# A hybrid encoder layer on one core: zero tile for the clock-raising passes, x rows first, and four blocks' queries normalised where they are used

## The chip, the cores and the metric

The kernel runs on one core of a Trainium2 chip. The time is the device time of one execution in microseconds; "before" and "after" are compared by it. The profile is that of one execution: TensorE (PE, with its weight loads PEld), VectorE (DVE), ScalarE (ACT), GpSimd (POOL) and SyncE (SP), whose queue issues the DMA transfers here. Each engine works through its own queue in order.

## The reference

One encoder layer with two head groups beside each other, on a prompt of 256 rows and a sample of 2048, each with 16 learned meta rows in front; the model dimension is 1024.

```python
h = rmsnorm(z, norm_w)
proj = jnp.einsum('bld,de->ble', h, w_in)
q, k, v, g_att, c_val, c_glu, g_conv = jnp.split(proj, SPLIT_IDX, axis=-1)
q = rmsnorm(q.reshape(B, L, N_HEADS, HEAD_DIM), q_norm_w)      # 8 heads of 64
k = rmsnorm(k.reshape(B, L, N_KV_HEADS, HEAD_DIM), k_norm_w)   # 2 KV heads
att = windowed_gqa(q, k, v, sink).reshape(B, L, W_ATT) * jax.nn.silu(g_att)
cnv = conformer_conv(c_val, c_glu, conv_w, conv_b, ln_w, ln_b) * jax.nn.silu(g_conv)
mixed = jnp.concatenate([att, cnv], axis=-1)
return z + jnp.einsum('ble,ed->bld', mixed, w_out)             # residual
```

`windowed_gqa` lets a row see the keys at a distance of at most 128 (with a penalty on the distance), all 16 meta keys, and a sink logit; `conformer_conv` is a GLU, a depthwise convolution of width 31, a layer norm over channels and a swish. Everything is float32.

## The kernel before

**Tiling.** The rows are cut into 18 blocks of 128 (2 of the prompt, 16 of the sample), in 6 groups of 3. A float32 product is made of three passes on TensorE (`PASSES`: high by high, high by low, low by high), so operands are split into a high part (`xh`, `ws`) and a low part (`xl`).

**Stages.** Up to about 550 us the projections run, one weight unit after the other over the row groups, with the convolution on VectorE beside them (`pj<-xh,ws`, `y<-us,cw,y`). Then attention and output projection run, one step per block and eight slots per step (`slot_step`), at first merged with the last projections: in each step the scores `S` of one block, the transposes `pT` and the weighted sums `O` of the block before it, and parts of the output products into two PSUM banks `yb0` and `yb1`. `add` in `product` adds a finished bank to a tile `yo` that holds the residual rows (`load_x`) or a partial sum; a bank goes on accumulating for the next output after that, so the next matmul into it has to come behind the add.

**Order.** A list scheduler with a simulated timeline sets the order on each engine, except for instructions kept in program order (`pinned`, `pin`, `keep_in_program_order`), and except that GpSimd, and in the last part TensorE too, follow an order written by hand. `later(k, f)` puts work off by k ticks. All DMAs are issued on SP's queue. They use eight semaphores in turn.

**The start.** `stats(i)` loads the rows `xn0` (16 meta rows) to `xn3` and takes their mean squares; POOL makes 1/rms of them and VectorE multiplies. TensorE transposes them (`turn0`, `xt<-ident,xn`). Between these, `busy` runs passes that only keep TensorE at work, 10, 5, 2 and 3 of them ahead of the rows 0 to 3, each of two records in the trace, on the identity matrix, which POOL makes. ScalarE then multiplies by the norm weights, held in `vec` (`split0`, `xh<-xt,vec`).

**Queries.** `q_group` makes the queries of a block, half of the heads (256 columns) at a time. In the merged stage ScalarE copies the raw product out of PSUM (`qr<-pj`), the 1/rms of each head (`rqq`) is worked out, and `fin` multiplies on VectorE (`qr<-qr,rqq`) and stores to the DRAM buffer `qd` (`qd<-qr`). For the second half of the last four blocks, 14 to 17, `fin` is put off by `put_off` (16 to 34 ticks), past the projections. In the attention stage, `load_q` loads a block's queries from `qd` (`q<-qd`), and `q_prep` transposes them (`qT`) and splits them.

Of the kernel before, what the change touches and what calls it, by code (L numbers as in the profile page):

```python
# [11 lines left out]
F32 = mybir.dt.float32  # L12
# [3 lines left out]
ALU = mybir.AluOpType  # L16
AX = mybir.AxisListType

P = 128
# [10 lines left out]
HD = 64  # L30
# [3 lines left out]
UW = 256  # L34
# [23 lines left out]
VSLOT = 3  # L58
# [83 lines left out]
def hymba_kernel(  # L142
# [11 lines left out]
    nc = tc.nc  # L154
# [5 lines left out]
    qd = dram.tile([NB, P, 512], F32, name="qd")  # L160
# [9 lines left out]
    ident = const.tile([P, P], F32, name="ident")  # L170
    make_identity(nc, ident)
    vec = const.tile([P, 30], F32, name="vec")
# [3 lines left out]
    lb = vec[:, 16:20]  # L176
    snk, msk, nsnk = vec[:, 22:24], vec[:, 24:28].rearrange("p (k i) -> p k i", k=2), vec[:, 28:30]
    vm = const.tile([P, 2, KV, P], F32R, name="vm")
    km = const.tile([P, KV, 2, NM], F32R, name="km")
    half = const.tile([P, 8], F32, name="half")  # L180
    nc.vector.memset(half, -0.5)
# [14 lines left out]
    def owe(ns):  # L196
        credit[0] -= ns

    def later(k, f):
        due.setdefault(clock[0] + k, []).append(f)  # L200
# [47 lines left out]
    kscale = cp.tile([P, 1], F32, tag="kscale", name="kscale", bufs=1)  # L248
# [106 lines left out]
    def load_v(b):  # L355
        vt[b] = [
            pool["a"].tile([P, KV, P], F32R, tag=f"v{k}", name=f"v{k}_{b}", bufs=VBUFS)
            for k in ("c", "m", "a", "b")[: 4 if kind(b) == "in" else 2]
        ]
        t = [x.rearrange("p a e -> p (a e)").bitcast(F32) for x in vt[b]]  # L360
        if kind(b) != "in":
            at = b - (kind(b) == "last")
            for k in range(2):
                nc.sync.dma_start(t[k], vd[at + k])
            return
        nc.sync.dma_start(t[0][QB:P], vd[b, 0 : P - QB])
        nc.sync.dma_start(t[0][0:QB], vd[b - 1, QC : QC + QB])
        nc.sync.dma_start(t[1][0:QB], vd[b, P - QB : P])
        nc.sync.dma_start(t[1][QB:QC], vd[b - 1, P - QB : P])
        nc.sync.dma_start(t[1][QC:P], vd[b + 1, 0:QC])  # L370
        nc.sync.dma_start(t[2][0:QC], vd[b - 1, 0:QC])
        nc.sync.dma_start(t[2][QC:XR], vmd)
        nc.sync.dma_start(t[3][0:NM], vmd)
        nc.sync.dma_start(t[3][NM:XR], vd[b + 1, QC:P])

    def load_q(b):
        qt[b] = pool["a"].tile([P, 4, P], F32, tag="q", name=f"q{b}")
        nc.sync.dma_start(qt[b].rearrange("p a e -> p (a e)"), qd[b])

    def presplit_wo(e):  # L380

# [105 lines left out]
    def pin(on):  # L487
        def wrap(f):
            def g(*a, **k):
                r = f(*a, **k)  # L490
                if on:
                    tc.keep_in_program_order(r)
                return r

            return g

        return wrap
# [319 lines left out]
    def slot_step(s_, slot):  # L817
        a, bb = s_, s_ - 1
        has_a, has_b = a < NB, 0 <= bb < NB
        steps = PLAN if has_b else []  # L820
        if slot == 0:
            if a + 1 < NB:
                load_q(a + 1)
                load_k(a + 1)
        if slot == 1 and has_b and s_ > 1:
            load_ga(bb)
        if slot == VSLOT and 0 < a < NB:
            load_v(a)
        t = 8 * s_ + slot
        with_rest(lambda: None)  # L830
        for f in acts.get(t, ()):
            f()
        if slot < len(steps) and steps[slot]:
            bank(bb, *steps[slot])
        for job in jobs.get(t, ()):
            product(*job)
        if has_a:
            scores(a, slot // 4, slot % 4)
        if slot == (3 if s_ == 1 else 5 if s_ == 3 else QSLOT) and a + 1 < NB:
            q_prep(a + 1)  # L840
        for job in late_jobs.get(t, ()):
            product(*job)
        tick(2400)
# [44 lines left out]
    if True:  # L888
# [3 lines left out]
        def pinned(op, yes=True):  # L892
            if yes:
                tc.keep_in_program_order(op)
# [294 lines left out]
        def q_group(ws, qi, g, after):  # L1189
            for b in range(3 * g, 3 * g + 3):  # L1190
                ps = proj_te(ws, g, blk_local(b)[1], P)
                late = phase[0] == 2
                raw = None
                tail = max(0, last_n[0] - (LTAGS_N - 4))
                put_off = 10 + 6 * tail if tail else 0
                if late:
                    raw = gp.tile([P, 4, HD], F32, tag="go" if b % 2 else "qs", name=f"qr{qi}_{b}")
                    nc.scalar.copy(raw, ps[:, :UW].rearrange("p (h e) -> p h e", e=HD))
                rq = head_norm(ps, P, 4, f"q{qi}_{b}", 2 * late + put_off)

                def fin(ps=ps, rq=rq, b=b, raw=raw):
                    tag = "go" if phase[0] == 2 and b % 2 else "qs"
                    qs = raw if raw is not None else gp.tile([P, 4, HD], F32, tag=tag, name=f"qs{qi}_{b}")
                    pin(late and not put_off)(nc.vector.tensor_tensor)(
                        qs,
                        qs if raw is not None else ps[:, :UW].rearrange("p (h e) -> p h e", e=HD),
                        rq.unsqueeze(2).to_broadcast([P, 4, HD]),
                        op=ALU.mult,
                    )
                    to = qd[b, :, UW * qi : UW * qi + UW]  # L1210
                    later(2 - late, lambda: nc.sync.dma_start(to, qs.rearrange("p h e -> p (h e)")))

                owe(340)
                later(1 + 2 * late + put_off, fin)
                tick(24 * 110)
                after(b)

# [70 lines left out]
        def busy(pt, n):  # L1288

            for _ in range(n):  # L1290
                tc.keep_in_program_order(nc.tensor.matmul(pt[:, :P], ident, ident, start=True, stop=True))  # L1291

        def turn0(i, d):

# [18 lines left out]
        preps = [Prep(g, False) for g in range(6)]  # L1313
        w01 = [weights(k) for k in range(2)]
        r = {0: stats(0)}
        nc.sync.dma_start(vec[:, 0:28], vecs)
        for i in (1, 2, 3):
            r[i] = stats(i)
        w01[0][0](nc.sync)
        w01[1][0](nc.sync)  # L1320
        nc.sync.dma_start(cw, conv_w)
        warmup = psum.tile([P, 512], F32, tag="a", name="warmup")
        for i in range(4):
            r[i]()
            o, rows = SEGS0[i]
            pinned(nc.vector.tensor_scalar(rows0[i][:rows], rows0[i][:rows], rstd[:rows, i : i + 1], None, op0=ALU.mult))
            busy(warmup, (10, 5, 2, 3)[i])
            for d in range(6):
                tc.keep_in_program_order(turn0(i, d))
        preps[0].alloc()  # L1330
# [10 lines left out]
                for i in range(4):  # L1341
                    turn0(i, 6 + q)

        nc.vector.tensor_scalar(nsnk, snk, -1.0, None, op0=ALU.mult)
        nc.vector.scalar_tensor_tensor(kscale, vec[:, 20:21], -(HD ** -0.5), vec[:, 21:22], op0=ALU.mult, op1=ALU.mult)

        def at_item_start(i, c, u, g):
            if (c, u, g) == (1, ORDER[0], CHUNKS[1][1]):
                nc.sync.dma_start(km.bitcast(F32), kmd)
                for r0 in range(0, P, NM):  # L1350
                    at = vm[r0 : r0 + NM, r0 // 64]
                    nc.sync.dma_start(at.rearrange("p a e -> p (a e)").bitcast(F32), vmd)
            if i == 6:
                nc.gpsimd.memset(vm.bitcast(F32), 0.0)
            if i == 0:
                for q in range(4):
                    w01[1][1](q, nc.gpsimd if q % 2 else nc.vector)
                for k in (4, 5, 6):
                    r[k]()
            if i == 1:  # L1360
                later(1, preps[1].first)
                later(1, preps[1].alloc)
                later(1, lambda: preps[1].scale(0))
                for q in range(4):
                    if q < 3:
                        later(1, lambda q=q: preps[1].scale(q + 1))
                    later(1, lambda q=q: preps[1].split(q))
                later(1, lambda: conv(0, U_C[0], 0))
                for k in range(7, 10):
                    later(1, lambda k=k: later(1, stats(k)))  # L1370
                for q in range(4):
                    later(2, lambda q=q: preps[2].load(q))
            if i == I2:
                later(1, preps[2].first)
                later(1, preps[2].alloc)
                later(1, lambda: preps[2].scale(0))
                for q in range(4):
                    if q < 3:
                        later(1, lambda q=q: preps[2].scale(q + 1))
                    later(1, lambda q=q: preps[2].split(q))  # L1380
                later(1, lambda: conv(0, U_C[1], 0))
# [17 lines left out]
        for i, (c, u, g) in enumerate(items):  # L1399
# [39 lines left out]
            if (c, u) == (0, ORDER[-1]):  # L1439
                p = preps[g + 3]  # L1440
# [85 lines left out]
```

## Time and profile before

| | us |
|---|---|
| runs | 933.9, 935.42, 935.51; median 935.42 |
| the profiled execution | 935.46, its span 933.4 |
| PE busy | 926.0 (99%) |
| DVE busy | 786.3 (84%) |
| ACT busy | 447.6 (48%) |
| POOL busy | 350.5 (38%) |

The span runs from the first to the last instruction of the core; the time has 2.06 us more around it. A row of the timeline gives the start and the length in us, engine, line, operation, output<-inputs and shapes, and in brackets how long the engine stood idle before it and for whom. A row of a table of stretches gives the stretch, its length, the busy time of PE, PEld, DVE, ACT and POOL (with counts), the granted clock of TensorE, the DMA engines' share and GB/s. "DMA to landing" is the time from a transfer's issue on SP until its data are there.

### The profile page before, as it was taken

Reading aid. Unit: us, or ns where it says so; the run is one execution under the profiler, and the core shown is the slowest. Engines: PE = TensorE matmul, PEld = TensorE weight load, DVE = VectorE, ACT = ScalarE, POOL = GpSimd, SP = SyncE. Lnnn points to the kernel's source line nnn. Section 1 sums busy time; section 2 is a strip of 40 time slices with the busy share of each in tenths; the row PEclk is TensorE's granted clock in tenths of the full one; section 3 lists DMA queues with packets and bytes.
Section 4 is the critical chain, followed back from the end, with each engine's and each line's share of the span. In section 5 each row is a group of like instructions: output and inputs, shape, how many; then the busy total and the mean of one; then the engine's idle time right before and its main releaser. Section 6 shows DMA issues by size and latency. Waiting matters only on the chain.

```text
span 933.4 us, 16976 instructions
## 1 busy us (share of the span) xinstructions
PE 926.0 (99%) x5742; PEld 877.0 (94%) x5742; DVE 786.3 (84%) x1380; ACT 447.6 (48%) x1237; POOL 350.5 (38%) x538
## 2 busy tenths in 40 slices
PE   9999999999999999999999999999999999999998
PEld 8999999999999999999999999988888888888887
DVE  5799999989988899999996564689788888887884
ACT  7441222153447750011111356677667676776772
POOL 3420100075675310000000453676664556455652
PEclk9999999999999999999999999999999999999999
DMA  8579685488465472223333688998566566576431
GB/s 299 181 226 360 243 287 186 156 272 311 121 211 176 155 290 91 91 99 110 117 116 116 196 268 265 384 361 251 169 171 187 169 200 167 171 187 190 139 96 47
DMA packets 154183, 182.79 MB, mean 196 GB/s; under 512 B 48784, under 2 KB 114656, under 8 KB 153968
## 3 DMA queue, kind: packets, MB, share of 16 engines
q1 hardware_dynamic: 154096, 181.71, 60.0%
q8 instruction: 45, 0.74, 0.3%
q14 instruction: 42, 0.34, 0.1%
HBM read 115.81 MB, written 65.85 MB: 195 GB/s over the span
## 4 chain that ended last, share of the span: by engine, by line
PE 97%; DVE 1%; ACT 1%; POOL 1%; issue 0%; DVEq 0%; POOLq 0%
PE pj L1050 43%; PE yb L755 20%; PE pj L1066 16%; PE O L644 5%; PE S L490 4%; PE pT_c L610 2%; PE pT_m L610 2%; PE pT_x L610 1%; PE warmup L1291 1%; PE lnu L287 1%; PE lnt L263 1%; PE qT L490 1%; PE xt L1298 0%; DVE xt L959 0%; DVE y L1131 0%
## 5 line engine op out<-in xcount | busy, mean ns | idle before, releaser
L1050 PE MATMUL pj<-xh,ws 128*128 128x384 f32 (+1 forms) x1536 | 395.4, 338 | 0.1
L1131 DVE SCALAR_TENSOR_TENSOR y<-us,cw,y 128x1167 f32<-128x1167 f32 (+2 forms) x258 | 333.5, 1348 | 0.9
L1050 PEld LDWEIGHTS pj<-xh,ws 128*128 128x128 f32 x1536 | 280.9, 188 | 0.4 <-ACT xh L1306 0.4
L1050 PE MATMUL pj<-xl,ws 128*128 128x384 f32 (+1 forms) x768 | 261.4, 341 | 0.2 <-DVE xl L988 0.2
L1066 PE MATMUL pj<-ws,xh 128*128 128x256 f32 (+1 forms) x880 | 165.4, 284 | 0.7 <-ACT sqq L1179 0.4
L1050 PEld LDWEIGHTS pj<-xl,ws 128*128 128x128 f32 x768 | 144.3, 188 | 0.5 <-DVE xl L988 0.5
L1066 PEld LDWEIGHTS pj<-ws,xh 128*128 128x128 f32 (+1 forms) x880 | 136.5, 187 | 1.4 <-issue 1.0
L755 PE MATMUL yb<-wo,rest 128*128 128x512 f32 (+1 forms) x498 | 132.9, 400 | 0.5 <-DVE rest L490 0.5
L1066 PE MATMUL pj<-ws,xl 128*128 128x256 f32 (+1 forms) x440 | 123.8, 281 | 0.0
L755 PEld LDWEIGHTS yb<-wo,rest 128*128 128x128 f32 x498 | 86.8, 189 | 16.0 <-DVE rest L490 0.9
L580 POOL TENSOR_SCALAR sb<-sb,es 128x304 f32<-128x304 f32 (+4 forms) x144 | 73.0, 525 | 58.4 <-PE pT_x L610 20.6
L1165 ACT ACTIVATE go<-pj 128x384 f32<-128x384 f32 x48 | 23.5, 490 | 147.4 <-PE pj L1050 143.2
L185 POOL TENSOR_SCALAR ssk<-ssk 128x2 f32<-128x2 f32 x18 | 11.8, 657 | 208.2 <-ACT sqk L1179 205.2
L562 ACT ACTIVATE sb<-sb,nm 128x304 f32<-128x304 f32 (+4 forms) x144 | 77.2, 536 | 22.1 <-DVE nm L550 20.2
L550 DVE CUSTOM_DVE_ANT_0 sb<-S,bias,vec 128x304 f32<-128x304 f32 (+4 forms) x144 | 73.3, 510 | 11.4 <-PE S L490 10.4
L1066 PEld LDWEIGHTS pj<-ws,xl 128*128 128x128 f32 (+1 forms) x440 | 82.1, 187 | 0.3
L185 POOL TENSOR_SCALAR ssq<-ssq 128x4 f32<-128x4 f32 (+2 forms) x55 | 27.9, 507 | 99.3 <-ACT xn L913 72.8
L490 PEld LDWEIGHTS S<-kw,q 128*128 128x128 f32 x288 | 52.2, 188 | 11.1 <-ACT rest L490 0.3
L490 PE MATMUL S<-kw,q 128*128 128x304 f32 (+4 forms) x288 | 62.3, 299 | 0.0
L755 PE MATMUL yb<-wo,ptiles 128*128 128x512 f32 x216 | 59.9, 407 | 0.0
L490 POOL TENSOR_TENSOR at<-at,ga 128x256 f32<-128x256 f32 x36 | 27.0, 750 | 79.0 <-DVE at L666 79.0
L766 DVE TENSOR_TENSOR yo<-yb,yo 128x512 f32<-128x512 f32 (+1 forms) x55 | 37.1, 674 | 14.7 <-PE yb L755 14.5
(166 smaller groups left out, 1439.7 us busy)
## 6 DMA issues: line engine op xcount, KB each, us to landing
wd<-ws SPq DMA_DIRECT2D x36, 512.0 KB, 5.8
ws<-wd SPq DMA_DIRECT2D x36, 512.0 KB, 6.1
wraw<-in_w_in SPq DMA_DIRECT2D x52, 256.0 KB, 6.3
xn<-in_z SPq DMA_DIRECT2D x18, 512.0 KB, 5.3
gd<-go SPq DMA_DIRECT2D x48, 192.0 KB, 2.9
yo<-in_z SPq DMA_DIRECT2D x36, 256.0 KB, 3.4
wo<-wod SPq DMA_DIRECT2D x18, 512.0 KB, 7.7
out_y<-yo SPq DMA_DIRECT2D x35, 256.0 KB, 2.3
```

Source lines behind the costliest of these rows:

```text
L185: nc.gpsimd.tensor_scalar(src, src, scale, eps, op0=ALU.mult, op1=ALU.add)
L490: r = f(*a, **k)
L550: nc.vector.tensor_tensor_reduce(out=sb[:, n, c0:c1], in0=ps[:, 0:w], in1=cst["bias"][:, kv, at + c0 : at + c1], scale=1.0, scalar=nsnk[:, ...
L562: nc.scalar.activation(sb[:, n, c0:c1], sb[:, n, c0:c1], AF.Exp, bias=nm[:, n : n + 1], scale=-1.0, accum_out=rs[:, n : n + 1],)
L580: nc.gpsimd.tensor_scalar(sb[:, k, a0:a1], sb[:, k, a0:a1], es[:, k : k + 1], 1.0, op0=ALU.mult, op1=ALU.mult)
L610: nc.tensor.transpose(pt[: c1 - c0, n, :], sbt[b, kv][:, n, c0:c1], ident)
L644: nc.tensor.matmul(opj[b, kv][:, n0:n1], t, p, start=(k == "c" and i == 0), stop=(k == "x" and i == len(work) - 1),)
L755: nc.tensor.matmul(ps[:, :n], x[mi][:, i, :], w[wi], start=((name, e) in OPENS and k == 0), stop=(done and e == es[-1] and k == 2), skip_g ...
L766: nc.vector.tensor_tensor(y, ps[:, :n], y, op=ALU.add)
L1050: nc.tensor.matmul(ps[:, :n], ws[:, d, wi, P * half_i : P * half_i + P], x[xi][:, d, o : o + n], start=(k == 0), stop=(k == 3 * ND - 1),)
L1066: nc.tensor.matmul(ps[:rows, :UW], x[xi][:, d, o : o + rows], ws[:, d, wi, :], start=(k == 0), stop=(k == 3 * ND - 1),)
L1131: op = nc.vector.scalar_tensor_tensor(y[:, yo + o0 : yo + o1], u[:, o0 + k : o1 + k], cw[:, j, k : k + 1], y[:, yo + o0 : yo + o1], op0=AL ...
```

## The change

- The passes of `busy` read `idle`, 128x128 elements of the tile `vm`, which VectorE sets to zero as its first work. The first group has 15 passes instead of 10 (30 records instead of 20). The memset of `vm` on POOL covers the remaining 384 columns and is pinned to a later place.
- On SP the load of `vec` stands behind the four loads of x rows. The two operations that make `nsnk` and `kscale` of it are pinned.
- For the second half of blocks 14 to 17, `keep` stores the raw queries one tick after the copy, and `rqq` is kept. `scale_q` multiplies on VectorE, in place, in the tile that `load_q` has loaded. `fin` and its multiply are not used for these four.

```diff
--- before.py
+++ after.py
@@ -176,6 +176,8 @@
     lb = vec[:, 16:20]
     snk, msk, nsnk = vec[:, 22:24], vec[:, 24:28].rearrange("p (k i) -> p k i", k=2), vec[:, 28:30]
     vm = const.tile([P, 2, KV, P], F32R, name="vm")
+    idle = vm[:, 0, 0].bitcast(F32)
+    nc.vector.memset(idle, 0.0)
     km = const.tile([P, KV, 2, NM], F32R, name="km")
     half = const.tile([P, 8], F32, name="half")
     nc.vector.memset(half, -0.5)
@@ -376,6 +378,13 @@
     def load_q(b):
         qt[b] = pool["a"].tile([P, 4, P], F32, tag="q", name=f"q{b}")
         nc.sync.dma_start(qt[b].rearrange("p a e -> p (a e)"), qd[b])
+
+    raw_q = {}
+
+    def scale_q(b):
+        qi, rq = raw_q[b]
+        q = qt[b].rearrange("p a e -> p (a e)")[:, UW * qi : UW * qi + UW].rearrange("p (h e) -> p h e", e=HD)
+        nc.vector.tensor_tensor(q, q, rq.unsqueeze(2).to_broadcast([P, 4, HD]), op=ALU.mult)
 
     def presplit_wo(e):
 
@@ -826,6 +835,8 @@
             load_ga(bb)
         if slot == VSLOT and 0 < a < NB:
             load_v(a)
+        if slot == VSLOT and a + 1 in raw_q:
+            scale_q(a + 1)
         t = 8 * s_ + slot
         with_rest(lambda: None)
         for f in acts.get(t, ()):
@@ -1201,7 +1212,7 @@
                 def fin(ps=ps, rq=rq, b=b, raw=raw):
                     tag = "go" if phase[0] == 2 and b % 2 else "qs"
                     qs = raw if raw is not None else gp.tile([P, 4, HD], F32, tag=tag, name=f"qs{qi}_{b}")
-                    pin(late and not put_off)(nc.vector.tensor_tensor)(
+                    pin(late)(nc.vector.tensor_tensor)(
                         qs,
                         qs if raw is not None else ps[:, :UW].rearrange("p (h e) -> p h e", e=HD),
                         rq.unsqueeze(2).to_broadcast([P, 4, HD]),
@@ -1210,8 +1221,15 @@
                     to = qd[b, :, UW * qi : UW * qi + UW]
                     later(2 - late, lambda: nc.sync.dma_start(to, qs.rearrange("p h e -> p (h e)")))
 
+                def keep(rq=rq, b=b, raw=raw):
+                    nc.sync.dma_start(qd[b, :, UW * qi : UW * qi + UW], raw.rearrange("p h e -> p (h e)"))
+                    raw_q[b] = (qi, rq)
+
                 owe(340)
-                later(1 + 2 * late + put_off, fin)
+                if put_off:
+                    later(1, keep)
+                else:
+                    later(1 + 2 * late, fin)
                 tick(24 * 110)
                 after(b)
 
@@ -1288,7 +1306,7 @@
         def busy(pt, n):
 
             for _ in range(n):
-                tc.keep_in_program_order(nc.tensor.matmul(pt[:, :P], ident, ident, start=True, stop=True))
+                tc.keep_in_program_order(nc.tensor.matmul(pt[:, :P], idle, idle, start=True, stop=True))
 
         def turn0(i, d):
 
@@ -1313,9 +1331,9 @@
         preps = [Prep(g, False) for g in range(6)]
         w01 = [weights(k) for k in range(2)]
         r = {0: stats(0)}
-        nc.sync.dma_start(vec[:, 0:28], vecs)
         for i in (1, 2, 3):
             r[i] = stats(i)
+        nc.sync.dma_start(vec[:, 0:28], vecs)
         w01[0][0](nc.sync)
         w01[1][0](nc.sync)
         nc.sync.dma_start(cw, conv_w)
@@ -1324,7 +1342,7 @@
             r[i]()
             o, rows = SEGS0[i]
             pinned(nc.vector.tensor_scalar(rows0[i][:rows], rows0[i][:rows], rstd[:rows, i : i + 1], None, op0=ALU.mult))
-            busy(warmup, (10, 5, 2, 3)[i])
+            busy(warmup, (15, 5, 2, 3)[i])
             for d in range(6):
                 tc.keep_in_program_order(turn0(i, d))
         preps[0].alloc()
@@ -1341,8 +1359,12 @@
                 for i in range(4):
                     turn0(i, 6 + q)
 
-        nc.vector.tensor_scalar(nsnk, snk, -1.0, None, op0=ALU.mult)
-        nc.vector.scalar_tensor_tensor(kscale, vec[:, 20:21], -(HD ** -0.5), vec[:, 21:22], op0=ALU.mult, op1=ALU.mult)
+        pinned(nc.vector.tensor_scalar(nsnk, snk, -1.0, None, op0=ALU.mult))
+        pinned(
+            nc.vector.scalar_tensor_tensor(
+                kscale, vec[:, 20:21], -(HD ** -0.5), vec[:, 21:22], op0=ALU.mult, op1=ALU.mult
+            )
+        )
 
         def at_item_start(i, c, u, g):
             if (c, u, g) == (1, ORDER[0], CHUNKS[1][1]):
@@ -1351,7 +1373,7 @@
                     at = vm[r0 : r0 + NM, r0 // 64]
                     nc.sync.dma_start(at.rearrange("p a e -> p (a e)").bitcast(F32), vmd)
             if i == 6:
-                nc.gpsimd.memset(vm.bitcast(F32), 0.0)
+                pinned(nc.gpsimd.memset(vm.bitcast(F32).rearrange("p h k e -> p (h k e)")[:, P:], 0.0))
             if i == 0:
                 for q in range(4):
                     w01[1][1](q, nc.gpsimd if q % 2 else nc.vector)
```

The new order changes on four engines. On SP, in the stage where the last projections run beside the first attention steps, the rows are, before from the load of `gc2` on, and then after, from behind the first wo2 transfer on (`wo` are split weights of the output projection, `wod` their buffer in DRAM, `yo1<-in_z` a load of residual rows; "x2" is two transfers in a row):

```order
L467 DMA gc2_6987<-gd_64 128x4x128
L457 DMA wo2_6597<-wod_71 128x1024 x2
L1211 DMA qd_63<-qr1_12_6411 128x256
L457 DMA wo2_6597<-wod_71 128x1024
L457 DMA wo3_6657<-wod_71 128x1024
L474 DMA yo1_6694<-in_z 128x512
L457 DMA wo3_6657<-wod_71 128x1024 x2
L1211 DMA qd_63<-qr1_13_6456 128x256
L378 DMA q4_7037<-qd_63 128x512
L457 DMA wo5_6881<-wod_71 128x1024
L457 DMA wo4_6780<-wod_71 128x1024
L350 DMA kw1_5913<-kd_65 128x4x32
```

```order
L1225 DMA qd_63<-qr1_14_6530 128x256
L1222 DMA qd_63<-qr1_12_6417 128x256
L466 DMA wo2_6605<-wod_71 128x1024 x2
L466 DMA wo3_6666<-wod_71 128x1024 x3
L1225 DMA qd_63<-qr1_15_6583 128x256
L1222 DMA qd_63<-qr1_13_6462 128x256
L1225 DMA qd_63<-qr1_16_6633 128x256
L380 DMA q4_7045<-qd_63 128x512
L466 DMA wo5_6891<-wod_71 128x1024
L466 DMA wo4_6790<-wod_71 128x1024
L1225 DMA qd_63<-qr1_17_6693 128x256
L483 DMA yo1_6704<-in_z 128x512
```

The four raw stores have moved here from further back in the queue, and the load of yo1 has moved from ahead of the second wo3 transfer to behind the first of wo4; the stores of blocks 12 and 13 and the load of q4 stood behind it or just ahead of it before.

On VectorE at the same stage (`sb<-S` is a maximum of scores, `pT` a transposed tile, `rest` the place of low parts):

```order
L625 TENSOR_TENSOR ptiles_6207<-pT1_c_0_6793,ptiles_6207 128x512
L766 TENSOR_TENSOR yo1_6694<-yb0_6725,yo1_6694 128x512
L490 TENSOR_TENSOR rest_6754<-temp1_6768,rest_6754 128x256
L490 TENSOR_TENSOR rest_6754<-cn0_6262,rest_6754 128x256
L490 TENSOR_TENSOR ptiles_6207<-cn0_6262,ptiles_6207 128x256
L666 TENSOR_TENSOR at0_6761<-O0_1_6736,tmp0_1_6858 64x256 x2
L625 TENSOR_TENSOR ptiles_6207<-pT1_m_0_6831,ptiles_6207 128x512
```

```order
L634 TENSOR_TENSOR ptiles_6213<-pT1_m_0_6841,ptiles_6213 128x512
L559 ISA sb1_5931,nm2_0_6808<-S2_0_1_6852,bias_5915,vec_77 128x208
L559 ISA nm2_0_6808 128x1
L499 TENSOR_TENSOR rest_6764<-cn1_6264,rest_6764 128x256
L628 SCALAR_TENSOR_TENSOR ptiles_6213<-pT1_x_0_6880,vec_77,ptiles_6213 128x128 x2
L499 TENSOR_TENSOR rest_6764<-at0_6771,rest_6764 128x256
L775 TENSOR_TENSOR yo1_6704<-yb0_6735,yo1_6704 128x512
L559 ISA sb1_5931,nm2_0_6808<-S2_0_2_6888,bias_5915,vec_77 128x240
```

The add of yb0 to yo1 has moved from behind the split of pT1_c_0 to behind the split of pT1_x_0 and rest<-at0. On TensorE, the next matmul into yb0 and what it waits for, before and after (the row ahead of it is the transpose pT1_x_0):

```order
L490 MATMUL S2_0_1_6842<-kw0_5912,q2_2_6647 128x208 x2
L644 MATMUL O1_0_6854<-ptiles_6207,vc_1_6633 128x512 x2
L606 MATMUL pT1_x_0_6870<-ident_72,pm1_0_6715 128x128 [waits PE_49,Pool_49]
L755 MATMUL yb0_6725<-wo1_6429,ptiles_6207 128x512 [waits Activation_49]
L755 MATMUL yb0_6725<-wo1_6429,ptiles_6207 128x512
L755 MATMUL yb0_6725<-wo1_6429,ptiles_6207 128x512 [waits DVE_49]
```

```order
L499 MATMUL S2_0_1_6852<-kw0_5918,q2_2_6656 128x208 x2
L653 MATMUL O1_0_6864<-ptiles_6213,vc_1_6642 128x512 x2
L615 MATMUL pT1_x_0_6880<-ident_72,pm1_0_6725 128x128 [waits PE_49,Pool_49]
L764 MATMUL yb0_6735<-wo1_6435,ptiles_6213 128x512 [waits DVE_49,Activation_49]
L764 MATMUL yb0_6735<-wo1_6435,ptiles_6213 128x512 x2
L764 MATMUL yb0_6735<-wo2_6605,ptiles_6213 128x512 [waits DMAHW6_49]
```

The first of its three passes now waits for VectorE too. The multiplies of `scale_q` stand on VectorE in the later attention steps; the one of block 16 after the change (the others stand likewise, behind the maxima S12_0_2, S13_0_2 and S15_0_2):

```order
L559 ISA sb1_5931,nm14_0_9668<-S14_0_2_9737,bias_5915,vec_77 128x304
L559 ISA nm14_0_9668 128x1
L387 TENSOR_TENSOR q16_9897<-q16_9897,rqq1_16_6639 128x256
L775 TENSOR_TENSOR yo1_6704<-yb1_6736,yo1_6704 128x512
L559 ISA sb1_5931,nm14_0_9668<-S14_0_3_9768,bias_5915,vec_77 128x304
```

It stands between a maximum and the add that followed that maximum before.

## The prediction, made before the changed kernel had run

> **What bounds the kernel now.** I read the page's head first, then the chain of waits, then a table of stretches, then the timeline of each engine at the places that the change touches, and last the DMA issues there with their time to landing.
>
> ```profile
> span 933.4 us, 16976 instructions
> PE 926.0 (99%) x5742; PEld 877.0 (94%) x5742; DVE 786.3 (84%) x1380; ACT 447.6 (48%) x1237; POOL 350.5 (38%) x538
> ...
> PE 97%; DVE 1%; ACT 1%; POOL 1%; issue 0%; DVEq 0%; POOLq 0%
> ```
>
> TensorE is busy 926.0 of 933.4 us and carries 97% of the chain that ended last. So other engines' work costs something only where it makes TensorE wait, and a gain is to be had only at the few places where TensorE waits now. The sum below is made against the profiled execution: a span of 933.4 us and a time of 935.46, 2.06 us more, which I carry along. The median of the runs, 935.42, is 0.04 below it. Against this kernel's spread I call 0.2% (1.87 us) the least difference that can be told: faster is below 933.5, slower above 937.3.
>
> **Part 1, the start.**
>
> ```profile
> 0.88 0.53 POOL L1354 MEMSET vm<- 128x512 f32 x1
> 1.79 4.64 PE L1291 MATMUL warmup<-ident 128*128 128x128 f32 x20 [1.79 <-POOL ident masks.py:199]
> 7.11 2.50 PE L1291 MATMUL warmup<-ident 128*128 128x128 f32 x10
> 9.40 1.46 PE L1298 MATMUL xt<-ident,xn 128*128 128x128 f32 x6
> 10.68 0.62 PE L1291 MATMUL warmup<-ident 128*128 128x128 f32 x4
> 11.79 0.83 PE L1291 MATMUL warmup<-ident 128*128 128x128 f32 x6
> 12.46 0.82 PE L1298 MATMUL xt<-ident,xn 128*128 128x128 f32 x6
> ...
> 10.57 0.75 DVE L1326 TENSOR_SCALAR xn<-xn,rstd 128x1024 f32<-128x1024 f32 x1 [0.72 <-POOL rstd L186]
> 12.78 1.08 ACT L1306 ACTIVATE xh<-xt,vec 128x400 fp32r<-128x400 f32 x2 [2.66 <-PE xt L1298]
> ...
> 0.81 0.07 DVE L181 MEMSET half<- 128x8 f32 x1 [0.81 <-PEq L1515]
> 1.19 0.41 SPq L1316 DMA_DIRECT2D vec<-in_vecs  x1
> ```
> ```profile
> L322 DVE MEMSET sb<- 128x32 f32 x9 | 0.5, 85 | 0.0
> ```
>
> TensorE's first work waits for the identity, which POOL has done at 1.79 behind its 0.53 us memset. Now it waits for a 128x128 memset that VectorE does first, from 0.81 on. No row has that memset; 8 columns took 0.065 us and 32 took 0.085, which makes 0.0008 us a column and so an estimate of 0.17: TensorE begins at about 1.0, 0.8 us earlier. A warm-up record takes (9.40 - 7.11) / 10 = 0.229 us while the clock is low and (12.46 - 11.79) / 6 = 0.112 when it is high. The rise came at about 10.6: six transposes took 1.28 us from start to start before it. The first burst, 4.6 us from 1.79, didn't bring it; the second, 3.5 us long when it came, did. Ten more records add 2.29 us at the low pace, so the first burst now lasts from 1.0 to 7.87, 6.9 us, and the rise should fall inside it, between 4.5 (3.5 us in) and its end.
>
> Walked from there at the high pace (six small transposes 0.45 by estimate, ten records 1.12, six transposes 0.65, four records 0.45, six transposes 0.65, six records 0.67), the last transposes begin at 11.87 if the rise comes at the end of the burst: 0.6 us earlier than 12.46. If it comes earliest, they are held by the last normalised rows. These were ready at 11.32 and come about 0.45 us earlier, at 10.87, since the vec load (0.41 us, and the gap behind it) no longer stands ahead of the x loads on SP: a gain of 1.6. I take the middle, 1.0. If the zero passes don't raise the clock at all, the ten records are cost, and 0.8 us of earlier start against 2.29 more leaves a loss of up to 1.5; with the rise where it was, at 10.6, what stands behind is walked at the high pace and the loss is about 0.7. ScalarE's xh, which waits for the last transposes at 12.78, and all behind it move by the same amount. Vec lands a microsecond later and is used only there; the two small operations on it (0.17 and 0.15 us) go behind a split whose successor has slack. I cost these at nothing (0.3 if that cover is gone), as I do POOL's remaining memset, which runs beside matmuls.
>
> A rule bears on this. The Trainium skill, "TensorE: Matmul & The Clock Gate", section "What's actually happening", has a free-running activity window of 3.41 us, and the clock goes up behind one busy window. By that rule a burst of 4.6 us may miss a whole window, as the first did here, and one of 6.9 holds one nearly always; with the rise of before at 10.6 the window edge would be at 7.2 and the gain about 0.85 instead of 1.0.
>
> **Part 2, the raw query stores and the residual load behind them.** The raw queries are stored at once, so five query stores now stand in the densest stretch of transfers, and on SP the residual load yo1 is issued behind loads of wo3, q4, wo5 and wo4 that it used to precede. On VectorE the add that uses it moves behind the split of pT_x and rest<-at0.
>
> ```profile
> 600.00:620.00 20.00, 19.38 (x126) 16.89 (x126) 16.75 (x48) 14.71 (x43) 11.46 (x28) 1.00 1.05 393
> ```
> ```profile
> 604.18 0.91 SPq L474 DMA_DIRECT2D yo<-in_z  x1
> ...
> 612.41 0.68 DVE L766 TENSOR_TENSOR yo<-yb,yo 128x512 f32<-128x512 f32 x1
> 615.29 1.63 PE L755 MATMUL yb<-wo,ptiles 128*128 128x512 f32 x6
> 617.83 0.61 DVE L490 TENSOR_TENSOR rest<-at,rest 128x256 fp32r<-128x256 f32 x1
> ...
> 605.27 0.37 ACT L1198 COPY qr<-pj 128x256 f32<-128x256 f32 x1 [0.67 <-PE pj L1066]
> ```
> ```profile
> DMA to landing us min/median/max: 7.5/7.5/7.5
> ```
> ```profile
> yo<-in_z SPq DMA_DIRECT2D x36, 256.0 KB, 3.4
> wo<-wod SPq DMA_DIRECT2D x18, 512.0 KB, 7.7
> ```
>
> Between 600 and 620 us the DMA engines are full (share 1.05, 393 GB/s), so what stands ahead on the queue is time. yo1 was issued at 604.18 and landed 7.5 us later, at 611.7, and the add ran at 612.41. Newly ahead of it are two more wo3 pieces, one of wo5 and one of wo4 (512 KB each), q4 (128x512 f32, as yo: 256 KB), and five query stores of 128x256 f32, 128 KB each: 2944 KB, or 3.01 MB, at 393 GB/s 7.7 us. So it lands at about 619.4, and the add (0.68) ends at 620.0. This add reads bank yb0, and the next matmul into that bank, TensorE's row at 615.29, must wait for it: it carries a wait on VectorE that it didn't have. Behind it TensorE's queue stands: 620.0 - 615.29 = 4.75 us, with nothing to fill it. Queued behind the add on VectorE are the maximum of the next scores and the next splits; TensorE produces their inputs only behind the same matmul, so they cost nothing more. Loads behind the five stores on SP come up to 1.7 us later (0.66 MB at 393 GB/s), less than TensorE's own delay.
>
> Both ends: even with the data there, the add comes behind rest<-at0, which ended at 618.44; with the earlier add (0.6) and one maximum (0.4) no longer ahead of it that is 617.45, the add ends at 618.1, and TensorE waits 2.8 us. At the top, if the transfers don't come earlier with TensorE's 1.0 us, the wait is 5.75. I take 4.75: it rests on the nearest rows, the landing of this very load.
>
> The rule that would speak against this is in the Trainium skill, "DMA: Bandwidth & Descriptors", section "Queues, rings and completion order": descriptors are consumed in ring order, but data may complete out of it. By that, a small load could land ahead of larger ones and the wait would shrink towards 2.8 and the sum to 939.2. The trace disagrees so far: the landing of 7.5 us for 256 KB, on an almost equal footing with the 7.7 of the 512 KB pieces, speaks for a queue.
>
> **Part 3, scaling the loaded queries.** The multiply now stands on VectorE behind a wait for the q load, one step before the block is used, right behind a maximum of the scores; everything on VectorE behind it waits for that load.
>
> ```profile
> L490 DVE TENSOR_TENSOR qr<-qr,rqq x14: 411/422/955, 569.7 to 675.6; 128x256 f32<-128x256 f32 x14
> ```
> ```profile
> L378 SPq DMA_DIRECT2D q<-qd x4: 430/934/1605, 801.9 to 857.1; - x4
> DMA to landing us min/median/max: 2.9/3.8/4.9
> ```
> ```profile
> L378 SPq DMA_DIRECT2D q<-qd x1: 1605/1605/1605, 819.9 to 819.9; - x1
> DMA to landing us min/median/max: 4.0/4.0/4.0
> ```
> ```profile
> L378 SPq DMA_DIRECT2D q<-qd x1: 430/430/430, 839.9 to 839.9; - x1
> DMA to landing us min/median/max: 4.9/4.9/4.9
> ```
> ```profile
> 822.64 1.05 DVE L490 TENSOR_TENSOR ptiles<-cn,ptiles 128x256 fp32r<-128x256 f32 x1 [1.34 <-ACT ptiles L490]
> 825.66 0.69 DVE L625 TENSOR_TENSOR ptiles<-pT_c,ptiles 128x512 fp32r<-128x512 f32 x1
> 826.70 0.62 PE L644 MATMUL O<-ptiles,vc 128*128 128x512 f32 x2
> 841.24 0.69 DVE L766 TENSOR_TENSOR yo<-yb,yo 128x512 f32<-128x512 f32 x1 [1.31 <-PE yb L755]
> 843.54 0.69 DVE L625 TENSOR_TENSOR ptiles<-pT_c,ptiles 128x512 fp32r<-128x512 f32 x1
> 846.01 0.62 PE L644 MATMUL O<-ptiles,vc 128*128 128x512 f32 x2
> ```
>
> For q15: issued at 819.9, landed 823.9, multiply (median 0.42) done at 824.3, where VectorE had gone on at 822.64: 1.7 us late. The split of pT_c at 825.66 then ends at about 827.9, and the second matmul of O at 826.70, which uses it, would have begun at 827.0: 0.9 us of waiting, of which I take 0.8, since a small gap ahead of the split is used up. For q16: landed 844.8, done 845.2, VectorE 4.0 late, the split ends near 847.8, the second O matmul would have begun at 846.3: 1.5 us. For q14 and q17, with shorter landings, I take nothing, and at most 0.9 each as for q15. Sum 2.3; ends 0 (the lateness is eaten by VectorE's gaps of 1.3 us elsewhere in the step before TensorE sees it) and 4.1 (twice 0.9 more).
>
> **Part 4, the multiplies that go.** Four of the 14 above leave VectorE between 621 and 676.
>
> ```profile
> 639.33 0.41 DVE L490 TENSOR_TENSOR qr<-qr,rqq 128x256 f32<-128x256 f32 x1
> 641.43 0.30 PE L606 MATMUL pT_x<-ident,pm 128*128 128x128 f32 x1 [0.32 <-POOL sb L580]
> ```
>
> TensorE's wait of 0.32 us at 641.43 hangs on a chain through VectorE that runs behind the multiply at 639.33, so it goes. The other three have no wait behind them in the trace. I take 0.4, between 0 and 0.8 (two such waits).
>
> **The sum.** 935.46 - 1.0 + 4.75 + 2.3 - 0.4 = 941.1 us.
>
> **Rivals.**
> (a) The clock falls in the long wait. No row shows TensorE idle this long after its start, so the price comes from the start's rows: at the low clock work takes about twice as long, until a burst of 3.5 to 6.9 us has raised it again, which loses 1.7 to 3.4 us: 942.8 to 944.5, 943.6 in the middle. Against it: 4.75 us is hardly longer than the shortest such burst. The same section on the clock gate lets it fall after one idle window; a wait of 4.75 holds a whole window of 3.41 in 4 of 10 phases.
> (b) The multiplies on the loaded queries cost nothing: 938.8. For it, VectorE's gaps; against it, its unbroken row from 822.64 to the split.
> (c) The zero passes don't raise the clock, so the change doesn't do what it says: +0.7 instead of -1.0, 942.8. For it, a first burst of 4.6 us that did nothing; against it, one of 3.5 that did.
> (d) On the other side: the matmul at 615.29 doesn't wait for the add. That needs an add that is done by 615.29, so a load landed by 614.6 and an add ahead of rest<-at0, or a wait that an earlier row of VectorE already fulfils. Then term two is 0: 936.4, not slower by more than can be told. Against it: the load's place and the add's are fixed in the queues.
>
> **How the numbers follow.** The forecast's own case has 0.47 (939.5 to 942.5 by its terms), (a) 0.18, (b) 0.16, (c) 0.07, (d) 0.07, and 0.05 is for what I have not seen. The range goes from 937.3, which leaves (d) out, to 944.5, the top of (a). Faster needs (d) together with costless multiplies or something unseen, 0.05; no difference, most of (d) and a little of (b), 0.08; slower 0.87.
>
> **What would show it.** In the new trace: warm-up from about 1.0, its records going from 0.23 to 0.11 us within the first burst, and the last transposes 0.6 to 1.6 us earlier; a gap of TensorE of 3 to 6 us ahead of yb<-wo1,ptiles near 615, put down to VectorE's add, with yo1 landing near 619; gaps of 0.8 and 1.5 us ahead of the second matmuls of O that stand at 827.0 and 846.3 now; no wait near 641. I am wrong if that matmul begins without a gap, if yo1 lands in 8 us, or if the clock runs low behind the gap.

## The result

The changed kernel takes 942.98 us (median of its six executions) against 934.82 for the kernel before: the ratio is 1.0086, with a 95% interval of 1.0072 to 1.0101. It is slower by some 8 us. One of the six took 4177.95 us at a mean granted clock of 0.208, which no run here explains; the ratio leaves it out, and the other five take 941.58 to 944.73, with a median of 942.75. The profiled execution took 941.58 us, 6.1 more than the profiled one of before, and is the fastest of the five.

The head of its page and the shares of the chain of waits:

```profile
span 939.8 us, 16999 instructions
PE 928.2 (99%) x5752; PEld 877.0 (93%) x5752; DVE 784.4 (83%) x1381; ACT 446.9 (48%) x1237; POOL 352.6 (38%) x538
...
PE 85%; DMA 6%; DVE 5%; ACT 1%; POOL 1%; issue 1%; SPq 1%; DVEq 0%; POOLq 0%; ACTq 0%
```

TensorE's work is nearly the same, but the chain now goes through DMA (6%) and VectorE (5%), which carried 0% and 1% of it. The list of waits names two of the places (who waited for whom, us in total, times, longest):

```profile
DVE q L387 <- DMA q<-qd: 13.0, 4, 4.1
PE yb L764 <- DVE yo L775: 4.3, 1, 4.3
```

**The start**, in the timeline:

```profile
0.83 0.17 DVE L180 MEMSET vm<- 128x128 f32 x1 [0.83 <-PEq L1537]
1.05 5.19 PE L1309 MATMUL warmup<-vm 128*128 128x128 f32 x30 [1.05 <-DVE half L183]
6.18 0.54 PE L1316 MATMUL xt<-ident,xn 16*128 16x16 f32 x6
10.96 0.88 PE L1316 MATMUL xt<-ident,xn 128*128 128x128 f32 x6
11.33 1.08 ACT L1324 ACTIVATE xh<-xt,vec 128x400 fp32r<-128x400 f32 x2 [1.32 <-PE xt L1316]
```

The memset took 0.17 us, TensorE begins at 1.05, 30 records took 5.13 us instead of the 6.9 of the low pace, so the clock rose inside the burst, and the last transposes begin at 10.96 instead of 12.46: 1.5 us earlier than in the profiled execution of before.

**The wait at yb0**, on TensorE, VectorE and SP, then two stretches with TensorE's granted clock (third column from the right):

```profile
613.74 0.27 PE L615 MATMUL pT_x<-ident,pm 128*128 128x128 f32 x1
618.34 2.53 PE L764 MATMUL yb<-wo,ptiles 128*128 128x512 f32 x6 [4.33 <-DVE yo L775]
...
615.90 0.96 DVE L499 TENSOR_TENSOR rest<-at,rest 128x256 fp32r<-128x256 f32 x1
617.50 0.69 DVE L775 TENSOR_TENSOR yo<-yb,yo 128x512 f32<-128x512 f32 x1 [0.64 <-DMA yo<-in_z]
...
612.03 0.33 SPq L483 DMA_DIRECT2D yo<-in_z  x1
```
```profile
615.00:620.00 5.00, 1.66 (x5) 1.34 (x6) 2.56 (x5) 0.62 (x3) 4.34 (x8) 0.88 1.06 384
620.00:625.00 5.00, 5.00 (x23) 4.23 (x22) 1.62 (x6) 1.25 (x4) 1.29 (x1) 0.78 1.07 352
```

The six records from 618.34 took 2.53 us where they took 1.63 before, and the granted clock, 1.00 in before from 600 to 630 us, is 0.88 and then 0.78: the clock fell at the end of the wait. A stretch at half clock that gives these two means is 1.2 + 2.2 = 3.4 us long.

**The multiplies on the loaded queries**, on VectorE, and TensorE behind the second and the fourth:

```profile
827.77 0.47 DVE L387 TENSOR_TENSOR q<-q,rqq 128x256 f32<-128x256 f32 x1 [2.84 <-DMA q<-qd]
847.67 0.42 DVE L387 TENSOR_TENSOR q<-q,rqq 128x256 f32<-128x256 f32 x1 [3.09 <-DMA q<-qd]
867.18 0.43 DVE L387 TENSOR_TENSOR q<-q,rqq 128x256 f32<-128x256 f32 x1 [4.06 <-DMA q<-qd]
...
831.29 0.50 PE L653 MATMUL O<-ptiles,vc 128*128 128x512 f32 x1 [0.22 <-DVE ptiles L634]
869.92 0.50 PE L653 MATMUL O<-ptiles,vc 128*128 128x512 f32 x1 [0.92 <-ACT ptiles L633]
870.64 0.50 PE L653 MATMUL O<-ptiles,vc 128*128 128x512 f32 x1 [0.23 <-DVE ptiles L634]
```

VectorE stands at each of them until its load has landed, and TensorE waits in two of the four steps.

Where the time went can be followed by matching TensorE's rows one by one and taking the difference of their starts (after minus before): -1.5 us behind the last transposes of the start, -1.1 at 571 us, -1.5 at the matmul ahead of the wait (a wait of 0.64 behind the row that starts at 612.65 in before shrank to 0.23), +3.05 behind the wait, +4.6 when the clock is up again, +3.7 at 796, +4.5 behind q15's wait, +4.65 ahead of and +6.65 behind q17's, +6.84 at the end. So: start -1.52, all of it still there at the wait; wait 4.57; low clock 1.58; multiplies that went, and small waits, -0.94; late multiplies 3.15. The tail behind TensorE is 0.45 shorter, which makes 6.4 of span, and 0.3 less lies around the span.

### The profile page after: what moved, and what is told of

Same layout as the page of the kernel before. It is cut to its first block, busy times and chain, and to the rows that moved or that the text cites. A ratio compares the mean times of both kernels' runs of the same rounds, so it can differ in the third digit from the quotient of the medians.

```text
span 939.8 us, 16999 instructions
## 1 busy us (share of the span) xinstructions
PE 928.2 (99%) x5752; PEld 877.0 (93%) x5752; DVE 784.4 (83%) x1381; ACT 446.9 (48%) x1237; POOL 352.6 (38%) x538
## 4 chain that ended last, share of the span: by engine, by line
PE 85%; DMA 6%; DVE 5%; ACT 1%; POOL 1%; issue 1%; SPq 1%; DVEq 0%; POOLq 0%; ACTq 0%
PE pj L1061 41%; PE yb L764 16%; PE pj L1077 14%; PE O L653 4%; PE S L499 3%; DMA q<-qd 1%; PE pT_c L619 1%; PE pT_m L619 1%; PE pT_x L619 1%; DMA wo<-wod 1%; DVE xt L970 1%; PE lnu L289 1%; DMA cd<-zn 1%; DVE ptiles L634 1%; PE lnt L265 1%
## 5 line engine op out<-in xcount | busy, mean ns | idle before, releaser
L764 PEld LDWEIGHTS yb<-wo,ptiles 128*128 128x128 f32 x216 | 38.4, 191 | 12.0 <-issue 4.7
```

Of the source, the lines that this page charges most:

```text
L764: nc.tensor.matmul(ps[:, :n], x[mi][:, i, :], w[wi], start=((name, e) in OPENS and k == 0), stop=(done and e == es[-1] and k == 2), skip_g ...
```

## The experiments

### The start's part alone

The kernel before with the first and second point of the change (zero tile, 15 passes, x rows first), and the old handling of the queries.

```diff
-            busy(warmup, (10, 5, 2, 3)[i])
+            busy(warmup, (15, 5, 2, 3)[i])
...
-                tc.keep_in_program_order(nc.tensor.matmul(pt[:, :P], ident, ident, start=True, stop=True))
+                tc.keep_in_program_order(nc.tensor.matmul(pt[:, :P], idle, idle, start=True, stop=True))
```

> The start's part of the change alone, on the kernel before; the queries are handled as before. My theory: the zero passes raise the clock inside the first burst and the rows come 0.45 us earlier, so TensorE's first projection starts 1.4 us earlier, as in the changed kernel, and most of this stays to the end: 933.3 us against 934.8 before (ratio 0.9984). Rival: TensorE is earlier at the start but gives it back in the projections, where it waits for operands that don't come earlier: 934.8, no difference.

Measured: 934.27 against 934.46 of before, ratio 0.9995, interval 0.9986 to 1.0004. That is the rival's number. But the rival's reason isn't what the profile shows. Here TensorE's rows are 1.2 us earlier than in the profiled execution of before up to 593 us, and 0.95 earlier from there to the very end: only a fifth is given back.

```profile
1.05 6.18 PE L1293 MATMUL warmup<-vm 128*128 128x128 f32 x30 [1.05 <-DVE half L183]
7.17 0.54 PE L1300 MATMUL xt<-ident,xn 16*128 16x16 f32 x6
12.24 0.63 PE L1052 MATMUL pj<-xh,ws 128*128 128x400 f32 x2
```

The first burst took 1 us longer than in the changed kernel, so the clock rose later in it. And the runs of before spread: of the 27 beside this one, 8 took 935.0 to 935.9 and 19 took 933.8 to 935.0, and the profiled execution of before, 935.46, is of the later sort. Against it the start's part gains 1 us, against the median 0.2.

### Ten passes instead of 15

The same, with 10 passes on the zero tile in the first group.

> The start's part alone, on the kernel before, with 10 passes in the first group as before instead of 15 (20 records from 1.05 us, a first burst of about 4.3 us at the low pace). My theory: the clock's rise falls at a time that differs from run to run, and a burst of 4.3 us misses it in some: the runs spread over 1.5 to 2 us as before's do (933.8 to 935.9), against 1.0 us with 15, and the median is 934.2, about that with 15. Rival: the time of the rise doesn't matter, since the rows set the end of the start: no wider than with 15, 933.8 to 934.7.

Measured: 934.52 us, ratio 1.0 (0.9991 to 1.0009); 11 runs from 933.48 to 935.79, a spread of 2.3 us against 1.0 with 15 passes (933.71 to 934.71). The spread is the theory's.

```profile
1.05 4.64 PE L1293 MATMUL warmup<-vm 128*128 128x128 f32 x20 [1.05 <-DVE half L183]
6.46 2.50 PE L1293 MATMUL warmup<-vm 128*128 128x128 f32 x10
10.03 0.67 PE L1293 MATMUL warmup<-vm 128*128 128x128 f32 x4
12.81 0.63 PE L1052 MATMUL pj<-xh,ws 128*128 128x400 f32 x2
```

In this execution the first burst missed the rise, the ten records from 6.46 ran at the low pace, and the first projection comes at 12.81, 0.6 us later than with 15. It took 934.52 all the same, the median of its runs, so that a missed rise is what makes the slower runs is not shown.

### Two more profiles of the kernel before

> The kernel before once more, for a second profile of its start. My theory: the 27 runs of before fall into about 18 near 934.2 and 9 near 935.3, and the profile that I predicted from (935.46) is of the later sort, with the clock's rise at 10.6 us. A run near 934.2 has the rise inside or right behind the first burst and its first projection about 1 us earlier than 13.42. Rival: the rise is always at 10.6, and the two sorts differ elsewhere.

> As before_look_2, a third profile of the kernel before: the rise of the clock and the start of the first projection, beside its time.

They took 935.64 and 935.2 us. The first projection of the two, in this order:

```profile
13.69 0.63 PE L1050 MATMUL pj<-xh,ws 128*128 128x400 f32 x2
```
```profile
13.39 0.63 PE L1050 MATMUL pj<-xh,ws 128*128 128x400 f32 x2
```

By the pace of the records the clock rose at about 11.2 and 10.6, behind the second burst again, and the times go with it: 0.3 us more in the start, 0.4 in the time. But both executions are of the later sort, so no profile shows what the runs near 934.2 do at their start. That these have an earlier rise stays argued, not shown.

### The load of yo1 ahead of the raw stores

The changed kernel with the raw stores put off by as many ticks as the old multiply was:

```diff
-                    later(1, keep)
+                    later(1 + 2 * late + put_off, keep)
```

> The changed kernel, but the raw stores are put off by as many ticks as the old multiply and store were; the scheduler then issues them directly behind the load of yo1 instead of ahead of it, in the same dense stretch. My theory: the wait of 4.6 us ahead of the matmul into yb0 goes, and with it the fall of the clock (1.5 us in the profiled run, more in others), while the late multiplies still cost 3.2: 936.0 us, with a mean granted clock of 0.999 in every run. Rival: the five stores themselves hold up the loads behind them, so TensorE waits for a later load (wo3, wo4, wo5) instead: 939 or more.

Measured: 936.17 us against 934.46, ratio 1.0016 (1.0007 to 1.0024). The theory's number; every one of the 11 runs has a mean clock of 1.0. The matmul and the add:

```profile
614.19 0.27 PE L615 MATMUL pT_x<-ident,pm 128*128 128x128 f32 x1
614.21 1.64 PE L764 MATMUL yb<-wo,ptiles 128*128 128x512 f32 x6
...
611.39 0.69 DVE L775 TENSOR_TENSOR yo<-yb,yo 128x512 f32<-128x512 f32 x1
```

The add is back behind the split of pT1_c_0 and done before TensorE needs the bank. The stores are still in the dense stretch, 128 KB each. A wait of 0.8 us at 621 is all that could be theirs in this profile, and it isn't in that of the kernel with both edits below, which has the same stores at the same place. So it is the place of the load and of the add, with the low clock behind the wait, and not the transfers of the stores, that cost 1.0086 - 1.0016 = 0.70%, 6.5 us. The edit moves the load and the add together; which of the two makes the wait is not parted by it.

### The multiplies kept in program order

The changed kernel with one more word: the multiply is kept in the order of the program, which puts it a step later, at the place that the code gives it. The scheduler had taken it a step ahead.

```diff
-        nc.vector.tensor_tensor(q, q, rq.unsqueeze(2).to_broadcast([P, 4, HD]), op=ALU.mult)
+        tc.keep_in_program_order(nc.vector.tensor_tensor(q, q, rq.unsqueeze(2).to_broadcast([P, 4, HD]), op=ALU.mult))
```

> The changed kernel, with the multiplies on the loaded queries kept in program order, which puts each of them one step (18.5 us) later on VectorE, long behind the landing of its load. My theory: the waits for the loads go (13.0 us of VectorE's time) and TensorE's 3.2 us behind them; the wait at yb0 and the low clock stay: 939.8 us. Rival: VectorE is so full in these steps that four more operations cost TensorE as much wherever they stand: 942.5 to 943, as the changed kernel.

Measured: 940.8 us, ratio 1.0064 (1.0051 to 1.0076). Between the theory's 939.8 and the rival's 942.5, nearer to the theory; its interval overlaps that of the changed kernel. No wait for the q loads is left, and TensorE's rows are 6.61 us behind those of before at 797 and 6.56 at the end, so these steps cost nothing now. What was more than expected is the wait at yb0, 6.1 us by the rows in this profile, with a low clock behind it that costs 2.5 us more:

```profile
620.33 2.90 PE L764 MATMUL yb<-wo,ptiles 128*128 128x512 f32 x6 [5.88 <-DVE yo L775]
...
616.35 0.96 DVE L499 TENSOR_TENSOR rest<-at,rest 128x256 fp32r<-128x256 f32 x1
619.50 0.69 DVE L775 TENSOR_TENSOR yo<-yb,yo 128x512 f32<-128x512 f32 x1 [2.19 <-DMA yo<-in_z]
```
```profile
615.00:620.00 5.00, 0.00 (x0) 0.00 (x0) 2.81 (x7) 1.06 (x4) 4.78 (x8) 0.89 1.03 367
620.00:625.00 5.00, 4.67 (x12) 3.83 (x13) 0.66 (x3) 0.59 (x2) 1.27 (x1) 0.50 1.07 321
625.00:630.00 5.00, 5.00 (x28) 4.31 (x28) 2.68 (x9) 2.12 (x7) 0.55 (x2) 0.92 1.01 385
```

VectorE waits 2.19 us for yo1 here and 0.64 in the changed kernel: the load was issued at 614.19 instead of 612.03. The means of 0.89, 0.50 and 0.92 make a stretch at half clock of 1.1 + 5.0 + 0.8 = 6.9 us, twice as long as in the profile of the changed kernel. Its mean clock is 0.996 in all five runs.

### Both edits at once

> Both edits at once: the raw stores behind the load of yo1 and the multiplies kept in program order. My theory: what is left is the gain of the start and of the multiplies that went: 934.8 - 1.5 - 0.5 = 932.8 us (ratio 0.9979). Rival: as in the two runs apart, 936 or more.

Measured: 933.04 us against 934.46, ratio 0.9987 (0.9978 to 0.9996): the theory's number, and the one version here that is faster than the kernel before, by 1.4 us. Against the same with the early multiplies (936.17) the late place on VectorE is worth 3.1 us. The four multiplies in this kernel cost more time themselves (0.84 us in the mean instead of 0.43) and nobody waits for them:

```profile
L387 DVE TENSOR_TENSOR q<-q,rqq 128x256 f32<-128x256 f32 x4 | 3.4, 842 | 0.0
```

What it has over the start's part alone, 1.2 us by the medians (the intervals overlap), is made in part between 640 and 800 us: its rows go from 1.28 to 1.84 us ahead of those of before.

### Work in the wait

The changed kernel with 18 matmuls more in the wait, which repeat two sums into the same bank with the same result.

```diff
             bank(bb, *steps[slot])
+            if bb == 1 and steps[slot][0] == "x" and steps[slot][1] == 0:
+                for r in range(18):
+                    nc.tensor.matmul(
+                        opj[1, 0][:, 0:4], vt[1][0][:, 0], pv_st[1, "c", 0][r % 2],
+                        start=(r % 2 == 0), stop=False, skip_group_check=True,
+                    )
```

> The changed kernel with 18 more matmuls (the two of O1_0<-vc_1, nine times again, which gives the same sums) ahead of the matmul into yb0 that waits: 18 x 0.23 = 4.2 us of work in the wait of 4.6. My theory: the load and the add come as before, so the wait stays as long, but the clock doesn't fall behind it: the records behind it take 0.23 us apart and not 0.42, the mean granted clock is 0.999 or more, and the time is 941.5 less what lay between it and the runs with a lower clock: 940.0 median, 3 us below the changed kernel's 943.0, with the runs closer together. Rival: the slow records behind the wait are due to the crowded transfers or the weight loads there; then they stay slow, and the time is 943 or, where the added work outlasts the wait, up to 1 us more.

Measured: 941.7 us, ratio 1.008 (1.0067 to 1.0092). In the profile the theory holds:

```profile
613.39 4.44 PE L848 MATMUL O<-ptiles,vc 128*128 128x512 f32 x18
618.10 1.63 PE L764 MATMUL yb<-wo,ptiles 128*128 128x512 f32 x6 [0.26 <-DVE yo L775]
```
```profile
615.00:620.00 5.00, 4.74 (x22) 3.59 (x21) 2.25 (x6) 0.26 (x1) 4.05 (x6) 1.00 1.07 369
620.00:625.00 5.00, 5.00 (x30) 4.34 (x29) 2.93 (x10) 2.43 (x8) 1.57 (x2) 1.00 1.04 345
```

The matmul into yb0 is as late as before (4.7 us behind, from the row ahead of the wait to the row behind it), but the clock stays at 1.00 and the six records take 1.63 us, as in the kernel before; behind them nothing more is lost. So the slow records are the clock's. In the medians it is worth less than the 3 us that I expected, and its interval overlaps that of the changed kernel, whose five runs (941.6 to 944.7) have mean clocks of 0.995 to 0.998; here they are 0.998 to 1.0, with times from 940.4 to 943.6. The spread is no narrower, so the runs differ by more than the clock; the kernel with early multiplies and a high clock throughout (936.17) spreads over 2.8 us too, which could be the landing of the q loads. But the kernel with both edits, where nobody waits for them, spreads over 3.1 us, so this is not shown.

## Why the prediction was right, and where its sizes were off

Slower was forecast, at 941.1 us; 942.98 was measured, and the two largest terms, the wait at yb0 and the late multiplies, are the two that were named. But 942.98 lies above the 939.5 to 942.5 of the forecast's own case, at the foot of rival (a)'s 942.8 to 944.5. The sum put the clock behind the wait at nothing; the clock fell there, which the prediction itself had named as a sign of being wrong. On that step it was wrong, and the range held because it reached to the top of (a).

- **The start, -1.0.** In the profiles the mechanism came as described: TensorE at 1.05, the rise inside the first burst, the transposes 1.5 us earlier. As a term of the difference in medians it was too large: alone it is worth 0.2 us (0.9995). The step that failed is that it was priced against one profiled execution, which is one of the later third of before's runs. The rise doesn't come at one time: in the six profiles with 30 records the small transposes behind the burst begin at 6.12 to 7.17 us, though the first projection then begins at 11.98 to 12.24 in all six.
- **The wait at yb0, 4.75.** 4.57 by the rows, 4.33 shown as idle. yo1 landed at 617.5; the forecast, 619.4 moved by the start's 1.5, says 617.9, and the transfers issued from 600 to 620 us landed in the order of their issue. But the landing was the last release by 0.64 us only. VectorE came to the add at 616.86, 3.1 us behind the start of the transpose that stands ahead of TensorE's wait. So with the data there the wait would have been 3.7 us and not the 2.8 of the forecast's lower end, in part since rest<-at0, which stands ahead of the add, took 0.96 us instead of 0.61. The two causes lie over each other and don't add up: the landing alone, with the add at its old place, would have held the bank to the same 618.2. Both figures are worked out from the rows; no run moved one without the other.
- **The five stores.** They were counted as work ahead of the load. Behind it they cost between nothing and 0.8 us.
- **The late multiplies, 2.3.** 3.15 in the profile, 3.1 between two of the experiments. The places differ: q15 cost 0.8 (forecast 0.8), q16 nothing (1.5), q17 2.0 (nothing), and 0.2 more came behind each of q15 and q17. The step that failed is the use of before's landings for the changed kernel: q16's load took 4.9 us in before (4.5 to 4.9 in its three profiles) and 2.9 after, q17's 2.9 (in all three) and 4.7. Which load is the slow one changes with the kernel, so that the sum came out near is in part luck.
- **The multiplies that went, -0.4.** -0.94 in the profile between 623 and 796 us. The wait at 641 didn't go; it shrank from 0.48 to 0.23 us (excess between two rows' starts).
- **The rivals.** (a), the fall of the clock, had 0.18, and it came about in each of the five runs of the changed kernel by their mean clocks (0.995 to 0.998), where the prediction had reckoned with 4 phases in 10. Its price in the profile is 1.58 us, just under the 1.7 to 3.4 that it was given, and 2.5 us in the kernel with the multiplies in program order. The profiled execution has the highest mean clock of the five, 0.998; the other four have 0.995 or 0.996, and 0.996 goes with the 6.9 us at half clock of that other profile. So in these four the low stretch was probably about as long, and the price nearer to 2.5 us; this is argued from the mean clocks, for they have no profile. The reason against it, that 4.75 us is hardly longer than a burst that raises the clock, didn't hold. The Trainium skill, "TensorE: Matmul & The Clock Gate", section "What's actually happening", has the fall behind one idle window of 3.41 us; the low stretches of 3.4 and 6.9 us here agree with a window as their unit. (b), multiplies that cost nothing, fell with 936.17 against 933.04. (c), passes that don't raise the clock, fell with every profile of 30 records; with 20, one execution missed it. (d), no wait for the add, fell with the row at 618.34.

That the profiled execution, at 941.58, came within half a microsecond of the forecast is the work of misses that cancel: +1.58 by the clock and +0.85 by the late multiplies, -0.52 by the start with the small wait ahead of yb0, -0.18 by the wait, -0.54 by the multiplies that went, and -0.72 behind and around the span.

## What to carry to other kernels

When a transfer is moved in a full queue, look for the vector operation that uses it and for whoever waits behind that operation in order; here the later add by itself would have made 3.7 of the 4.3 us, and the later landing all of it, so mending one of the two would have gained little. Work that is put "where it is used" must stand behind its load by more than the load's spread; one step later on the same engine made 3.1 us of waiting vanish, and the scheduler had to be told. A TensorE wait of over 4 us cost the clock as well here (1.6 and 2.5 us in two profiles), and a gain at the start of a kernel has to be priced against several executions of before, not one.

## What the hardware showed that I had not expected

In the profiled execution the granted clock fell not in the wait but behind its end: TensorE was at work again at 618.34; its first three records are 0.31 us apart, those from 618.96 on 0.43, and those from 622.3 on 0.23, as in the kernel before. If idleness is judged over a stretch as long as the low one, 3.4 us, the one ahead of the fall held some 0.4 us of work, so a stretch need not be idle throughout to count as idle; this is an inference from one profile. In the kernel with the multiplies in program order the mean of 0.89 puts the fall at about 618.9, inside the longer wait that ended at 620.33, and the clock stayed low twice as long. And the end of the first burst, where the clock rises, differs by 1 us between six executions of one sort of start, of which 0.3 us is left at the first projection.
